# Slots, weight halves and token buffers at fixed places modulo 256 bytes

## The chip, the cores and the metric

One core of a Trainium2 chip runs the whole program. The metric is the device time of one execution in microseconds; the median of three runs stands for the kernel.

## The reference

The reference is one inference step of a decoder trunk with two layers, in float32, for a prompt of 512 tokens and for 8 sample tokens that share the weights. Each layer is a half-step SwiGLU feed-forward (FFN), a token mixer and another such FFN, each followed by a layer norm of `alpha*x + f(x)`.

```
swiglu_half(x) = 0.5 * ((silu(x @ wg) * (x @ wu)) @ wd)      # 1024 -> 2816 -> 1024
x = LN(alpha*x + swiglu_half(x))
x = LN(alpha*x + mixer(x))     # layer 0: retention (4 heads) beside RG-LRU; layer 1: causal pooling
x = LN(alpha*x + swiglu_half(x))
```

So there are four FFNs, one input and one output projection of the mixer of layer 0, and a small pooling mixer in layer 1. Outputs are the tokens and the new states.

## The kernel before, in words

Activations lie feature-major: 128 features of a chunk on the partitions, tokens along the free axis, 8 chunks. The 520 tokens are cut into two streams: stream 0 has the first 256 prompt tokens, stream 1 the other 256 and the 8 samples (`NN = (256, 264)`).

To keep float32 precision with fp32r products, each operand is split into a high part (rounded to fp32r) and a low part (the rest), and each product is made of three: high weight by high x, high weight by low x, low weight by high x (`emit`, line 533, calling `mm`, line 199; the matmuls stand at line 200). A unit of work is one output chunk of 128 columns: 8 (or 7) contraction chunks times three, so 24 (or 21) matmuls into one PSUM tile `ps`, for stream 0 with 256 columns and for stream 1 with 264. The two streams alternate, about six units apart, so each weight piece serves both.

The moving operands are of two kinds. For gate, up and mixer-input units they are the tiles `xh0`/`xh1` (high) and `xl0`/`xl1` (low), made in `alloc` (line 214) as constants of shape [128, 8, NN[s]]: a chunk stride of 1024 bytes in stream 0 and 1056 in stream 1. For down and mixer-output units they are hidden slots: `put_h` (line 846) and `ret_finish` (line 1138) take a slot as [128, 4, 264], rows high, low, high, low of two chunks, 1056 bytes apart in both streams (`hview`, line 836). In the rows below, xh and xl name the first kind, and `ps<-sl,sl` the second.

All slots are buffers of one pool of 36, each 1056 float32 wide (4224 bytes a partition), taken from its start by `slot` (line 119). A weight piece is up to 1024 float32 wide; it is loaded by a DMA from the SyncE queue into a slot (`load`, line 415), split in `prep` (line 427) into a high slot by ScalarE (line 178) and a low slot by VectorE (line 183), and then the raw slot is dropped. The order of the work is made at build time by a planner (`run`, line 501): it estimates the engines' times, and hands out slots by count. The number of slots that weights may hold (`wcap`, line 388) is the slot count less 10 in the FFNs, and a constant in the mixer and around the pooling; other work may take a slot when `can` (line 135) leaves a reserve.

The places in a partition follow from these sizes. The constants end at byte 57,920, so slot k starts at 57,920 + 4224k: 64 mod 256 for even k, 192 for odd k. The four x tiles start at 18,816, 27,008, 35,456 and 43,648, all 128 mod 256; stream 0's chunks all stay at 128, stream 1's step by 32. The chunks of a weight piece are 512 bytes apart. "Place 192/64" below says where high and low slot of a piece start, mod 256. The trace itself holds no addresses.

Of the kernel before, what the change touches and what calls it, by code (L numbers as in the profile page):

```python
# [8 lines left out]
F32 = mybir.dt.float32  # L9
F32R = mybir.dt.float32r  # L10
# [4 lines left out]
P = 128  # L15
DM = 1024
NCH = DM // P
# [4 lines left out]
NN = (HALF, HALF + NS)  # L22
# [15 lines left out]
QSCALE = 128.0 ** -0.5  # L38
GELU_C = math.sqrt(2.0 / math.pi)

NSLOT = 36
SLOTW = 1056
W_RESERVE = 5
N_RAW = 4
AHEAD = 5
# [46 lines left out]
class Build:  # L92
    def __init__(self, ctx, tc, ins, outs):
# [3 lines left out]
        self.cpool = ctx.enter_context(tc.tile_pool(name="cp", bufs=1))  # L97
        self.spool = ctx.enter_context(tc.tile_pool(name="sp", bufs=NSLOT))
        self.tpool = ctx.enter_context(tc.tile_pool(name="tp", bufs=2))
        self.pp = ctx.enter_context(tc.tile_pool(name="pp", bufs=5, space=bass.MemoryType.PSUM))  # L100
        self.pm = ctx.enter_context(tc.tile_pool(name="pm", bufs=3, space=bass.MemoryType.PSUM))
        self.free = NSLOT
        self.wused = 0
# [12 lines left out]
    def const(self, name, shape, dt=F32):  # L116
        return self.cpool.tile(shape, dt, tag=name, name=name)

    def slot(self, shape, dt=F32):
        assert self.free > 0, "no slot"  # L120
        self.free -= 1
        n = self.size(type("S", (), {"shape": shape}))
        assert n <= SLOTW
        t = self.spool.tile([P, SLOTW], dt, tag="slot", name=self.nm("sl"))
        v = t[:, :n]
        if len(shape) == 3:
            v = v.rearrange("p (a b) -> p a b", a=shape[1])
        elif len(shape) == 4:
            v = v.rearrange("p (a b c) -> p a b c", a=shape[1], b=shape[2])
        return v  # L130

    def drop(self, n=1):
        self.free += n
# [80 lines left out]
    def alloc(self):  # L214
        self.XE = [self.const(f"x{s}", [P, NCH, HALO + NN[s]]) for s in range(2)]
        self.XA = [t[:, :, HALO:] for t in self.XE]
        self.X = [[t[:, d, HALO:] for d in range(NCH)] for t in self.XE]
        self.XHA = [self.const(f"xh{s}", [P, NCH, NN[s]], F32R) for s in range(2)]
        self.XLA = [self.const(f"xl{s}", [P, NCH, NN[s]], F32R) for s in range(2)]
        self.XH = [[t[:, d, :] for d in range(NCH)] for t in self.XHA]  # L220
        self.XL = [[t[:, d, :] for d in range(NCH)] for t in self.XLA]
        self.H = [[None] * 4, [None] * 4]
        self.PT = [Tm(0.0), Tm(0.0)]
        self.SA, self.QA, self.M0, self.VA = [None] * 2, [None] * 2, [None] * 2, [None] * 2
        self.sm = self.const("small", [P, SMALL_W])
        self.ones_r = self.const("ones_r", [P, P], F32R)
        self.TL = self.const("tail", [P, NCH, PB + NS])
        self.XSM = self.const("xsm", [P, NCH, NS])
        self.b3 = self.const("b3", [P, NCH])
        self.UTAIL = self.const("utail", [P, 4, 3])  # L230
        self.UEND = self.const("uend", [P, 4, 3])
        self.HTAIL = [self.const(f"htail{s}", [P, 4]) for s in range(2)]
        self.US = self.const("us", [P, 4, NS])
        self.HS = self.const("hs", [P, 4, NS])
        self.SMP = self.const("smp", [P, 4, HEADS, NS])
        self.sp4 = self.const("sp4", [P, 4])
        self.pbs = self.const("pbs", [P, NCH])
        self.pss = self.const("pss", [P, NCH])
        self.one = self.const("one", [P, 1])
        self.tiny = self.const("tiny", [P, 1])  # L240
# [147 lines left out]
    def wcap(self):  # L388
# [4 lines left out]
        if self.idx[0] >= self.u_pool - 4 and self.idx[1] < self.u_pool + 8:  # L393
            return WCAP_P
        return NSLOT - WFF

# [30 lines left out]
    def prep(self, win=None):  # L427
        for wi, k in self.wanted(win or AHEAD + 1).items():
            if self.free < 2 or self.wused >= self.wcap():
                break  # L430
            w = self.wl[wi]
            if w["st"] != 1:
                continue
            if k > 0 and win is None and max(self.t_act, self.t_dve) > self.t_pe + 4.0:
                break
            T = Tm(w["traw"])
            if "full" in w:
                w["t"] = T.t
                w["st"] = 2
                self.nraw -= 1  # L440
                continue
            w["hi"] = self.slot([P, w["n"]], F32R)
            w["lo"] = self.slot([P, w["n"]], F32R)
            self.wused += 2
            raw = w["raw"][:]
            with self.prio(self.d_prep()):
                for c in range(0, w["n"], w["part"]):
                    cs = slice(c, c + w["part"])
                    self.act(T, w["hi"][:, cs], raw[:, cs])
                    if w is self.wl[0] and c == 0:  # L450
                        self.split(0, 0, Tm(0.0))
                    self.tt(T, w["lo"][:, cs], raw[:, cs], w["hi"][:, cs].bitcast(F32), ALU.subtract)
            w["t"] = T.t
            w["raw"] = None
            w["st"] = 2
            self.drop()
            self.wused -= 1
            self.nraw -= 1
            self.dma_ahead()
# [376 lines left out]
    def hview(self, s, k):  # L836
        t = self.H[s][k // 2]
        n = NN[s]
        j = 2 * (k % 2)
        return t[:, j, :n], t[:, j + 1, :n]  # L840

    def hfree(self, s):
        self.H[s] = [None] * 4
        self.drop(4)

    def put_h(self, T, s, k, h):
        if self.H[s][k // 2] is None:
            self.H[s][k // 2] = self.slot([P, 4, NN[1]], F32R)
        hi, lo = self.hview(s, k)
        self.act(T, hi, h)  # L850
        self.tt(T, lo, h, hi.bitcast(F32), ALU.subtract)
# [286 lines left out]
    def ret_finish(self, pr, s, T):  # L1138
        n = NN[s]
        B = self.RP[s]  # L1140
        yield from self.get(1)
        Q = self.slot([P, 4, NN[1]])
        ob, vv = B[:, 0:2, :n], B[:, 2:4, :n]
        sq, r0 = Q[:, 0:2, :n], Q[:, 2:4, :n]
        self.act(T, sq, ob, AF.Square)
        yield from self.pmget(2)
        yield ("pe", T)
        for e in range(2):
            pv = self.pmt()
            self.mm(pv[:, :n], self.s("ones"), sq[:, e, :], True, True)  # L1150
            T.t = self.t_pe + .1
            self.ts(T, vv[:, e, :], pv[:, :n], LN_EPS, ALU.add)
        self.pmfree += 2
        self.rstd(T, vv, r0, sq, vv)
        self.tt(T, ob, ob, vv, ALU.mult)
        yield ("v", None)
        while any(("sg", 2 * pr + e, s) not in self.flags for e in range(2)):
            yield ("w", None)
        yield from self.get(1)
        H = self.H[s][pr] = self.slot([P, 4, NN[1]], F32R)  # L1160
        for e in range(2):
            h = 2 * pr + e
            gn = self.s("gn_g")[:, h:h + 1]
            self.stt(T, ob[:, e, :HALF], ob[:, e, :HALF], gn, self.QK[h, s][:, 3, :], ALU.mult, ALU.mult)
            if s == 1:
                self.stt(T, ob[:, e, HALF:], ob[:, e, HALF:], gn, self.SMP[:, 3, h, :], ALU.mult, ALU.mult)
        hv = H[:, :, :n].rearrange("p (c two) n -> p two c n", two=2)
        hi, lo = hv[:, 0], hv[:, 1]
        self.act(T, hi, ob)
        self.tt(T, lo, ob, hi.bitcast(F32), ALU.subtract)  # L1170
        self.drop(4)
        if s == 1:
            self.drop(1 + pr)
        for h in (2 * pr, 2 * pr + 1):
            self.flags[("ret", h, s)] = T.t
            if s == 1:
                self.flags[("retdone1", h, 0)] = 0.0
                self.flags[("retdone1", h, 1)] = 0.0
# [235 lines left out]
```

## Time and profile before

| | us |
|---|---|
| three runs | 1850.99, 1851.36 (median), 1856.78 |
| profiled execution | 1856.6 |
| its span | 1854.8 |
| TensorE busy | 1816.8 (14727 matmul records) |
| VectorE busy | 909.8 |
| ScalarE busy | 688.3 |

The span runs from the first to the last instruction; a few us lie around it. Busy TensorE is not TensorE at its peak: records of matmuls overlap in time, and what counts is the distance from one start to the next. A window of one group (24 or 21 matmuls of one `ps` tile) has the group's first start and the next group's first start as its edges, so its length over 24 or 21 is that distance; its count of records is two higher than the group's, for the two matmuls before that are still in flight.

### The profile page before, as it was taken

To read this page: it belongs to the slowest core of one execution; us is meant where nothing else is said; L and a number is where in the kernel's file an instruction comes from. 1 tells how busy PE (TensorE), PEld (TensorE's weight loads), DVE (VectorE), ACT (ScalarE), POOL (GpSimd) and SP (SyncE) were. 2 spreads that over 40 slices of the span, in tenths; PEclk is the share of its full clock that TensorE was granted. 3 is DMA by queue.
4 is the path that set the end of the run, shared out by engine and by line. 5 is a ranking of instruction groups with operands and counts; after the bars stand their busy time and mean duration, and the time that the engine had idled before them with its cause. 6 is when DMAs were issued, how large, how long until landed. Compare 5 with 4: busy or idle time off the path is not lost.

```text
span 1854.8 us, 33820 instructions
## 1 busy us (share of the span) xinstructions
PE 1816.8 (98%) x14727; PEld 1791.7 (97%) x14727; DVE 909.8 (49%) x1629; ACT 688.3 (37%) x1208; POOL 2.1 (0%) x10
## 2 busy tenths in 40 slices
PE   8999999999899999999999999999999899999997
PEld 8999999999889999999999999999999799999997
DVE  5433333497655784333335833333347843333336
ACT  5422222275644463222223732222224742222223
POOL 0000000000000000000000000000000000000000
PEclk9999999999889999999999999999999999999998
DMA  7232232223043323222332323323259723223311
GB/s 259 92 92 86 87 102 84 76 80 103 13 146 97 126 82 92 92 86 90 99 89 85 113 81 93 96 85 100 77 80 97 71 84 99 91 84 99 96 31 47
DMA packets 77380, 170.74 MB, mean 92 GB/s; under 512 B 24368, under 2 KB 37168, under 8 KB 77232
## 3 DMA queue, kind: packets, MB, share of 16 engines
q1 hardware_dynamic: 77232, 168.58, 32.6%
q8 instruction: 115, 1.88, 0.4%
q14 instruction: 33, 0.27, 0.0%
HBM read 163.44 MB, written 5.12 MB: 91 GB/s over the span
## 4 chain that ended last, share of the span: by engine, by line
PE 88%; DVE 5%; ACT 5%; issue 1%; DMA 0%; SPq 0%; ACTq 0%; DVEq 0%
PE ps L200 85%; PE pm L200 3%; ACT sl L178 2%; DVE sl L183 2%; DVE sl L196 1%; DVE x L183 1%; ACT L685 1%; ACT L178 1%; ACT xh L178 1%; DVE xl L183 0%; DVE e L183 0%; DMA x<-in_xa 0%; ACT e L178 0%; ACT x L178 0%; DVE sl L968 0%
## 5 line engine op out<-in xcount | busy, mean ns | idle before, releaser
L200 PE MATMUL ps<-xh,sl 128*128 128x264 f32 (+1 forms) x6400 | 1177.1, 283 | 10.2 <-ACT xh L178 6.3
L200 PEld LDWEIGHTS ps<-xh,sl 128*128 128x128 f32 x6400 | 1000.1, 190 | 14.7 <-ACT xh L178 7.0
L200 PE MATMUL ps<-xl,sl 128*128 128x264 f32 (+1 forms) x3200 | 906.4, 284 | 3.6 <-DVE xl L183 3.3
L200 PEld LDWEIGHTS ps<-xl,sl 128*128 128x128 f32 x3200 | 607.3, 190 | 6.1 <-DVE xl L183 5.4
L200 PE MATMUL ps<-sl,sl 128*128 128x264 f32 (+1 forms) x4672 | 596.5, 285 | 4.1 <-DVE sl L196 4.0
L200 PEld LDWEIGHTS ps<-sl,sl 128*128 128x128 f32 x4672 | 577.3, 189 | 9.1 <-DVE sl L196 5.3
L178 ACT ACTIVATE sl<-sl 128x1024 fp32r<-128x1024 f32 (+8 forms) x371 | 349.0, 950 | 465.3 <-PE ps L200 421.2
L183 DVE TENSOR_TENSOR sl<-sl,sl 128x1024 fp32r<-128x1024 f32 (+3 forms) x320 | 374.1, 1174 | 243.3 <-ACT sl L178 222.9
L183 DVE TENSOR_TENSOR e<-sil,ps 128x256 f32<-128x256 f32 (+1 forms) x176 | 74.7, 424 | 305.4 <-PE ps L200 301.6
L196 DVE SCALAR_TENSOR_TENSOR x<-ps,x 128x256 f32<-128x256 f32 (+1 forms) x208 | 88.5, 427 | 249.1 <-PE ps L200 249.0
L178 ACT ACTIVATE sl<-e 128x264 fp32r<-128x264 f32 (+1 forms) x184 | 76.6, 416 | 282.5 <-DVE e L183 281.5
L178 ACT ACTIVATE sil<-ps 128x264 f32<-128x264 f32 (+1 forms) x176 | 67.1, 382 | 191.5 <-PE ps L200 190.8
L183 DVE TENSOR_TENSOR sl<-e,sl 128x264 fp32r<-128x264 f32 (+1 forms) x184 | 78.6, 427 | 60.2 <-ACT sl L178 60.1
L183 DVE TENSOR_TENSOR x<-x,sl 128x512 f32<-128x512 f32 (+2 forms) x136 | 87.1, 677 | 2.9 <-ACT sl L178 1.9
L178 ACT ACTIVATE e<-x 128x256 f32<-128x256 f32 (+1 forms) x87 | 35.1, 415 | 54.0 <-DVE x L196 53.7
L178 ACT ACTIVATE xh<-x,small 128x256 fp32r<-128x256 f32 (+1 forms) x64 | 35.1, 596 | 9.6 <-DVE x L183 9.5
L178 ACT ACTIVATE sl<-pm 128x256 f32<-128x256 f32 (+2 forms) x44 | 15.0, 364 | 57.7 <-PE pm L200 57.7
L183 DVE TENSOR_TENSOR xl<-x,xh 128x512 fp32r<-128x512 f32 (+1 forms) x40 | 27.6, 695 | 5.8 <-ACT xh L178 5.3
L183 DVE TENSOR_TENSOR sl<-sl,e 128x256 f32<-128x256 f32 (+1 forms) x63 | 26.8, 425 | 3.5 <-ACT e L178 2.2
L178 ACT ACTIVATE x<-x,small 128x256 f32<-128x256 f32 (+1 forms) x44 | 25.7, 596 | 4.5 <-DVE x L183 4.3
L178 ACT ACTIVATE e<-ps 64x256 f32<-64x256 f32 (+3 forms) x40 | 15.4, 384 | 26.2 <-PE ps L200 20.1
L183 DVE TENSOR_TENSOR sl<-sl,x 128x256 f32<-128x256 f32 (+1 forms) x54 | 23.0, 425 | 0.9
(115 smaller groups left out, 474.5 us busy)
## 6 DMA issues: line engine op xcount, KB each, us to landing
sl<-in_w SPq DMA_DIRECT2D x241, 512.0 KB, 3.7
sl<-in_w SPq DMA_DIRECT2D x64, 448.0 KB, 3.3
sl<-in_sret SPq DMA_DIRECT2D x4, 512.0 KB, 5.1
out_rets<-sl SPq DMA_DIRECT2D x4, 512.0 KB, 3.6
x<-in_xb SPq DMA_DIRECT2D x2, 528.0 KB, 9.2
out_y<-x SPq DMA_DIRECT2D x4, 264.0 KB, 2.3
x<-in_xa SPq DMA_DIRECT2D x4, 256.0 KB, 5.5
sl<-in_dec SPq DMA_DIRECT2D x2, 512.0 KB, 5.0
```

The source lines that it names most:

```text
L178: r = self.nc.scalar.activation(out, in_, func, scale=scale, **kw)
L183: r = self.nc.vector.tensor_tensor(out=out, in0=a, in1=b, op=op)
L196: self.nc.vector.scalar_tensor_tensor(out=out, in0=a, scalar=s, in1=b, op0=op0, op1=op1)
L200: self.nc.tensor.matmul(out, lhsT, rhs, start=start, stop=stop)
L685: self.nc.scalar.preload_act_table_set(LNEXP)
```

## The change

Slots become 1088 float32 wide (4352 bytes) and are 35 instead of 36. `slot` takes an offset. A high weight starts 32 float32 into its slot, a low one at its start. The x tiles of the high and low parts get chunk strides of 256 and 320 float32 (1024 and 1280 bytes). Hidden slots get row strides of 256 float32 at an offset of 16 in stream 0, and 264 at no offset in stream 1. The work itself, its engines and its shapes are the same.

```diff
--- before.py
+++ after.py
@@ -38,8 +38,12 @@
 QSCALE = 128.0 ** -0.5
 GELU_C = math.sqrt(2.0 / math.pi)
 
-NSLOT = 36
-SLOTW = 1056
+NSLOT = 35
+SLOTW = 1088
+XSTR = (256, 320)
+HSTR = (256, 264)
+HOFF = (16, 0)
+HIOFF = 32
 W_RESERVE = 5
 N_RAW = 4
 AHEAD = 5
@@ -116,18 +120,21 @@
     def const(self, name, shape, dt=F32):
         return self.cpool.tile(shape, dt, tag=name, name=name)
 
-    def slot(self, shape, dt=F32):
+    def slot(self, shape, dt=F32, off=0):
         assert self.free > 0, "no slot"
         self.free -= 1
         n = self.size(type("S", (), {"shape": shape}))
-        assert n <= SLOTW
+        assert off + n <= SLOTW
         t = self.spool.tile([P, SLOTW], dt, tag="slot", name=self.nm("sl"))
-        v = t[:, :n]
+        v = t[:, off:off + n]
         if len(shape) == 3:
             v = v.rearrange("p (a b) -> p a b", a=shape[1])
         elif len(shape) == 4:
             v = v.rearrange("p (a b c) -> p a b c", a=shape[1], b=shape[2])
         return v
+
+    def hslot(self, s):
+        return self.slot([P, 4, HSTR[s]], F32R, HOFF[s])
 
     def drop(self, n=1):
         self.free += n
@@ -215,8 +222,8 @@
         self.XE = [self.const(f"x{s}", [P, NCH, HALO + NN[s]]) for s in range(2)]
         self.XA = [t[:, :, HALO:] for t in self.XE]
         self.X = [[t[:, d, HALO:] for d in range(NCH)] for t in self.XE]
-        self.XHA = [self.const(f"xh{s}", [P, NCH, NN[s]], F32R) for s in range(2)]
-        self.XLA = [self.const(f"xl{s}", [P, NCH, NN[s]], F32R) for s in range(2)]
+        self.XHA = [self.const(f"xh{s}", [P, NCH, XSTR[s]], F32R)[:, :, :NN[s]] for s in range(2)]
+        self.XLA = [self.const(f"xl{s}", [P, NCH, XSTR[s]], F32R)[:, :, :NN[s]] for s in range(2)]
         self.XH = [[t[:, d, :] for d in range(NCH)] for t in self.XHA]
         self.XL = [[t[:, d, :] for d in range(NCH)] for t in self.XLA]
         self.H = [[None] * 4, [None] * 4]
@@ -439,7 +446,7 @@
                 w["st"] = 2
                 self.nraw -= 1
                 continue
-            w["hi"] = self.slot([P, w["n"]], F32R)
+            w["hi"] = self.slot([P, w["n"]], F32R, HIOFF)
             w["lo"] = self.slot([P, w["n"]], F32R)
             self.wused += 2
             raw = w["raw"][:]
@@ -845,7 +852,7 @@
 
     def put_h(self, T, s, k, h):
         if self.H[s][k // 2] is None:
-            self.H[s][k // 2] = self.slot([P, 4, NN[1]], F32R)
+            self.H[s][k // 2] = self.hslot(s)
         hi, lo = self.hview(s, k)
         self.act(T, hi, h)
         self.tt(T, lo, h, hi.bitcast(F32), ALU.subtract)
@@ -1157,7 +1164,7 @@
         while any(("sg", 2 * pr + e, s) not in self.flags for e in range(2)):
             yield ("w", None)
         yield from self.get(1)
-        H = self.H[s][pr] = self.slot([P, 4, NN[1]], F32R)
+        H = self.H[s][pr] = self.hslot(s)
         for e in range(2):
             h = 2 * pr + e
             gn = self.s("gn_g")[:, h:h + 1]
```

## Rows read from the trace of the kernel before

**Rows 1.** The profile page: engine shares, and TensorE's granted clock in 40 slices.
```profile
PE 1816.8 (98%) x14727; PEld 1791.7 (97%) x14727; DVE 909.8 (49%) x1629; ACT 688.3 (37%) x1208; POOL 2.1 (0%) x10
...
PEclk9999999999889999999999999999999999999998
```

**Rows 2.** The page's chain of waits, shares of the span by line.
```profile
PE ps L200 85%; PE pm L200 3%; ACT sl L178 2%; DVE sl L183 2%; DVE sl L196 1%; DVE x L183 1%; ACT L685 1%; ACT L178 1%; ACT xh L178 1%; DVE xl L183 0%; DVE e L183 0%; DMA x<-in_xa 0%; ACT e L178 0%; ACT x L178 0%; DVE sl L968 0%
```

**Rows 3.** Windows of FFN stretches: length; PE, PEld, DVE, ACT, POOL busy; clock, DMA share, GB/s.
```profile
60.00:340.00 280.00, 279.89 (x2353) 279.68 (x2352) 106.10 (x185) 78.14 (x122) 0.00 (x0) 1.00 0.29 89
...
700.00:1000.00 300.00, 300.00 (x2521) 300.00 (x2520) 112.53 (x170) 83.33 (x132) 0.00 (x0) 1.00 0.29 90
...
1530.00:1780.00 250.00, 250.00 (x2101) 250.00 (x2101) 89.68 (x134) 66.53 (x103) 0.00 (x0) 1.00 0.30 93
```

**Rows 4.** Windows, TensorE alone: one 256-column group on xh/xl each.
```profile
132.55:135.28 2.72, 2.72 (x26) 1.00 0.00 0
...
138.19:141.02 2.83, 2.83 (x26) 1.00 0.03 6
...
149.60:152.32 2.73, 2.73 (x26) 1.00 0.00 0
...
155.25:158.08 2.83, 2.83 (x26) 1.00 0.02 6
...
161.00:163.77 2.77, 2.77 (x26) 1.00 0.00 0
...
189.42:192.16 2.73, 2.73 (x26) 1.00 0.00 0
...
254.19:257.04 2.85, 2.85 (x26) 1.00 0.03 13
```

**Rows 5.** Groups by line and form: the fp32r products: busy, mean ns, idle before.
```profile
L200 PE MATMUL ps<-xh,sl 128*128 128x264 f32 x3200 | 616.3, 285 | 0.0
...
L200 PE MATMUL ps<-xh,sl 128*128 128x256 f32 x3200 | 596.2, 282 | 10.2 <-ACT xh L178 6.3 <-ACT sl L178 2.9 <-DVE sl L183 0.9
...
L200 PE MATMUL ps<-xl,sl 128*128 128x256 f32 x1600 | 451.5, 283 | 2.6 <-DVE xl L183 2.3
...
L200 PE MATMUL ps<-sl,sl 128*128 128x264 f32 x2336 | 304.8, 287 | 4.1 <-DVE sl L196 4.0
...
L200 PE MATMUL ps<-sl,sl 128*128 128x256 f32 x2336 | 301.2, 284 | 0.0
```

**Rows 6.** Windows of one 256-column group (21 matmuls) on hidden slots each.
```profile
212.07:214.58 2.50, 2.50 (x23) 1.00 0.00 0
...
222.91:225.36 2.45, 2.45 (x23) 1.00 0.00 0
...
233.64:236.15 2.51, 2.51 (x23) 1.00 0.06 24
```

**Rows 7.** Windows of one 264-column group each: three on xh/xl, the last on hidden slots.
```profile
163.77:166.67 2.90, 2.90 (x26) 1.00 0.51 158
...
169.42:172.34 2.92, 2.92 (x26) 1.00 0.59 163
...
186.53:189.42 2.89, 2.89 (x26) 1.00 0.50 159
...
241.54:244.12 2.58, 2.58 (x23) 1.00 0.58 167
```

**Rows 8.** Groups by line and form: the splits of a weight piece on VectorE and ScalarE.
```profile
L183 DVE TENSOR_TENSOR sl<-sl,sl 128x1024 fp32r<-128x1024 f32 x239 | 290.9, 1224 | 144.7 <-ACT sl L178 132.3 <-PE ps L200 11.8
...
L178 ACT ACTIVATE sl<-sl 128x1024 fp32r<-128x1024 f32 x239 | 249.9, 1055 | 323.5 <-PE ps L200 297.5 <-DVE sl L183 14.7 <-DMA sl<-in_w 11.2
```

**Rows 9.** Windows of the mixer stage.
```profile
400.00:500.00 100.00, 93.66 (x716) 90.56 (x715) 74.75 (x160) 65.66 (x124) 0.78 (x3) 0.95 0.14 49
...
500.00:600.00 100.00, 95.66 (x653) 87.96 (x652) 59.32 (x138) 45.52 (x98) 0.21 (x1) 0.90 0.37 118
```

## Prediction

> **What bounds the kernel now.** I read four views. [...] Then the chain of waits: TensorE's fp32r products (line 200 into ps) carry 85% of the span [rows 2]. So the time is, for the most part, a count of matmuls times the distance from one start to the next. Third, long FFN stretches with no stall: 280 us hold 2353 matmuls, 300 us hold 2521, 250 us hold 2101, which is 119.0 ns each [rows 3]. [...]
>
> Fourth, one output group per window. A group is 24 matmuls of one stream (8 chunks times three products); the count of 26 includes the last two of the group before, still in flight. All windows of rows 4 are the same form: 256 columns, moving operand xh or xl of the first half, clock 1.00, DMA share 0.00 to 0.03. Yet they take 2.72 to 2.85 us, that is 113.3 to 118.8 ns per matmul [rows 4]. What differs between them is which slots the weights lie in. The moving chunks of the first half start at 128 mod 256 bytes; a slot starts at 64 or at 192. From the order in which the program hands out slots, the high and low weights of the seven windows start at: 192/64 (132.55), 64/64 (138.19), 64/64 (149.60), 192/192 (155.25), 192/64 (161.00), 192/64 (189.42), 64/192 (254.19). Three places can do either: the two 64/64 windows show 117.9 and 113.8. Inside a group the starts hold a steady beat, quick (113.3 ns) or slow (117.8 or 118.8). 192/64 alone always ends in the quick beat, after at most nine matmuls of transition: 113.3, 115.4 and 113.8 ns here; over the whole trace the 42 such groups without a stall (the first starts at 15.4 us, the last at 1756.7) average 113.9, the other 135 about 116.2. DMA does not decide it: in the same trace matmuls with and without a transfer running differ by about 0.2 ns in each form.
>
> [...]
>
> **The change part by part.** Counts are from the groups by form: 3200 + 1600 matmuls of 256 columns on xh/xl, 2336 on hidden slots (32 of them are the pooling's), and the same again at 264 columns [rows 5].
>
> *Weight slots.* 4352 bytes is 17 times 256, so every slot starts at one place mod 256. The constants grow by 2 x 8 x 56 x 4 = 3584 bytes, 14 times 256, so that place is 64 as for slot 0 before. Low weights lie at 64, high ones 128 bytes on, at 192. This is the 192/64 place, for every piece. First half on xh/xl: the whole trace gives 115.9 ns before (the seven windows: 115.8); 113.9 plus the last transition into the next group is 114.2 after. 4650 undisturbed matmuls x 1.7 ns = 7.9 us gained.
>
> *Hidden slots, first half.* Before, the four rows of a slot are 1056 bytes apart from a start at 64 or 192, so starts wander over all places. The 21-matmul windows take 2.45 to 2.51 us, 116.7 to 119.5 ns [rows 6]; 118.4 over the trace. After, stride 1024 and offset 64 put every row at 128 mod 256: the same geometry as xh/xl, so I price it with the 192/64 rows, with a little more transition: 114.3. 2270 x 4.1 = 9.3 us gained.
>
> *Second half on xh/xl, 264 columns.* Before, chunks shift by 32 bytes mod 256 from one to the next; after, stride 1280 puts all eight at 128. The windows give 120.4 to 121.7 ns [rows 7], 121.1 over the trace. No row shows 264 columns at one place for a whole group. [...] Upper bound: the slowest row at 264 columns, 2.58/21 = 122.9. What speaks for the upper half: the first three matmuls of such a group do lie at 128, and in the window at 163.77, which is in place 192/64 and follows a quick group, their starts go 118, 121 and 121 ns apart in the records: the quick beat is left at once. So I take 120.7, near the rows: 4740 x 0.4 = 1.9 us gained; the ends are 21 gained and 9 lost.
>
> *Second half on hidden slots.* Stride stays 1056, the start becomes 64 always. Before: 122.9 ns in the window shown [rows 7], 121.9 over the trace. Places still wander: nothing, at the nearest rows; 1 ns either way is 2.3 us.
>
> *One slot less (36 to 35).* The FFN cap on weight slots is the slot count less 10, so 26 becomes 25; the caps of the mixer and pooling stages are constants and stay. What hides this is the lead: the split on ScalarE sat idle 297.5 us until TensorE gave a slot free, so it is the buffers, filled far ahead, that set its pace, while TensorE waited only 0.9 us for low weights at this form [rows 5, 8]. In the stretches of rows 3 a piece is split some 30 us before its first use; a slot is about 3 us of that. Cost: nothing. If the cover were gone, a piece's two split operations (1.06 + 1.22 us) would be late at stage edges only: I keep 0 to 4 us. No instruction or DMA is added or taken away, and the operations on DVE and ScalarE keep their sizes; SP's and POOL's queues are as they were. What is late next, when the FFN runs faster, is nothing: ScalarE and DVE are at 28 and 38% there and DMA at 0.29 to 0.30 [rows 3].
>
> *What does not gain in full.* In the mixer TensorE waits for other engines (93.7 of 100 us busy, clock 0.95 and 0.90 [rows 9]); about one matmul in nine is there, and of its 1.8 us I take back 1. Where pauses move, half-speed stretches move too: the clock of 0.90 over 100 us cost about 10 us, so a few us either way.
>
> Sum: -7.9 - 9.3 - 1.9 + 1 = -18 us. Against the profiled execution (1856.6 us, span 1854.8) this is 1838.5. That execution is 5.2 us above the median of 1851.4, near the highest of the three runs; the forecast goes by the median: 1851.4 - 18 = 1833 us, own range 1827 to 1841.
>
> **The rivals.**
> 1. *The second half falls into the quick beat as well.* With all chunks at one place its geometry is that of the first half. For: 192/64 draws in 256-column groups from any entry. Against: the 118, 121, 121 above. At 117 to 118.5 ns it gives 12 to 19 us in place of 1.9: about 1819 us.
> 2. *Slower: one place, but the wrong beat.* A fixed layout gives all groups one fate. If the entry from the changed 264-column groups locks the first half in the slow beat of 254.19 (118.8 ns), xh/xl lose 2.9 x 4650 = 13.5 us and hidden slots 0.4 x 2270 = 1: 1866 us. It decides when more than half of the groups lock (4.8 x 6920 ns = 33 us between none and all, against 18). Against: every 192/64 group of before came in from a 264-column one, in many phases, and none stayed slow.
> 3. *The places are not what I work out*, so that high and low lie at 64/192: xh/xl keep their 115.8, hidden slots gain about 2.6 ns: 1845 us. For: the trace shows no addresses. Against: both growths are multiples of 256.
> 4. *Addresses do not matter*, and the beats of before had another cause that followed the slots by chance: 1851 us, at most 4 more for the slot.
>
> **How the numbers follow.** Forecast 0.58, rival 1 0.22, rival 2 0.06, rival 3 0.08, rival 4 0.06. 0.3% is 5.6 us; a measurement here can hardly tell less from no change. Faster by more: the forecast and rival 1, rival 3 mostly (1845 is 6 us), 0.87. Within it: rival 4 and the rest of 3, 0.07. Slower: 0.06. The range takes in rival 1 to 1814 and rival 3 to 1847.
>
> **What would show it.** In the profile after: windows of one first-half group at 2.72 to 2.75 us in every FFN, on xh/xl and on hidden slots alike (24 matmuls), none at 2.83; the mean of one 256-column MATMUL down from 282 and 284 ns by some 3; stall-free FFN stretches at 117.6 ns per matmul (2380 in 280 us) instead of 119.0. Second-half xh/xl windows at 2.80 us would be rival 1. Wrong would be: first-half groups at 2.83 or more in steady state (rival 2), a mix of both as before (4), or TensorE waits for splits in the FFN (the slot).

## The result: slower, 1873.7 us against 1854.0

Four runs of the changed kernel gave a median of 1873.68 us (1868.27 to 1878.83), four of the kernel before beside them 1853.96; the ratio is 1.0106, 95% interval 1.0071 to 1.0142. The forecast was 1833 us, its range ended at 1847. The profiled execution of after took 1873.2 us, span 1871.5, against 1856.6 and 1854.8 before: 16.7 us of span to explain.

Two things happened at once. First, the places did what was forecast. Windows of one group each of after, TensorE alone (columns as in [rows 4]): three 256-column groups that follow a hidden 264-column group, one that follows a 264-column group on xh/xl, and then two 264-column groups, on hidden slots and on xh/xl:

```profile
131.54:134.28 2.74, 2.74 (x27) 1.00 0.51 145
137.22:139.95 2.73, 2.73 (x26) 1.00 0.33 126
142.89:145.62 2.73, 2.73 (x26) 1.00 0.30 60
205.10:207.87 2.77, 2.77 (x26) 1.00 0.28 61
128.60:131.54 2.94, 2.94 (x26) 1.00 0.04 14
207.87:210.76 2.89, 2.89 (x27) 1.00 0.25 100
```

The first-half group no longer takes 2.83 or 2.85 us as three of seven did in [rows 4]. From start to start of neighbouring matmul records, with distances above 135 ns counted as pauses (at a granted clock of 0.50 starts lie 220 ns apart, as from 338.3 to 342.7 us in after, and so count as pauses too), the whole trace gives (ns; number undisturbed in after):

```
                     before   after   undisturbed   change, us
256 on xh/xl         115.88   114.70      4655         -5.5
256 on hidden        118.36   115.13      2248         -7.3
264 on xh/xl         121.12   120.33      4677         -3.7
264 on hidden        121.95   122.21      2283         +0.6
pauses, in excess      41.7     73.9  (us)            +32.2
```

Matmuls that run undisturbed became 15.9 us cheaper, and pauses 32.2 us dearer: 16.3 of the 16.7 us.

Second, the pauses. Two FFN windows of after (columns as in [rows 3]):

```profile
100.00:350.00 250.00, 245.40 (x2052) 244.47 (x2051) 86.83 (x138) 64.47 (x105) 0.00 (x0) 0.99 0.28 88
700.00:1000.00 300.00, 295.43 (x2480) 294.64 (x2479) 101.69 (x158) 78.53 (x126) 0.00 (x0) 0.99 0.28 89
```

The second held 2521 matmuls, all of it busy, in [rows 3]; now it holds 2480. The page of after, shares, clock and chain of waits; before, the chain was 85% line 200 into ps (207 in after) and no load of weights stood among its lines [rows 1, 2]:

```profile
PE 1812.7 (97%) x14727; PEld 1784.1 (95%) x14727; DVE 894.7 (48%) x1629; ACT 683.1 (37%) x1209; POOL 3.4 (0%) x10
...
PEclk9999999999889999999999999999999999999998
...
PE ps L207 59%; DMA sl<-in_w 14%; ACT sl L185 7%; DVE sl L190 7%; PE pm L207 3%; DVE sl L203 2%; DVE x L190 1%; ACT L692 1%; DVE e L190 0%; ACT L185 0%; DVE x L203 0%; ACT e L185 0%; DVE xl L190 0%; DVE sl L975 0%; ACT xh L185 0%
```

Groups by line and form of after, against [rows 8, 5]: ScalarE's idle time before a 1024-wide split used to end with TensorE (297.5 of 323.5 us), and now ends with the load:

```profile
L185 ACT ACTIVATE sl<-sl 128x1024 fp32r<-128x1024 f32 x239 | 251.0, 1055 | 416.0 <-DMA sl<-in_w 393.5 <-PE ps L207 15.9 <-DVE sl L190 6.4
L185 ACT ACTIVATE sl<-sl 128x896 fp32r<-128x896 f32 x64 | 61.0, 953 | 182.0 <-DMA sl<-in_w 169.4 <-PE ps L207 12.6
...
L190 DVE TENSOR_TENSOR sl<-sl,sl 128x1024 fp32r<-128x1024 f32 x239 | 291.5, 1224 | 397.8 <-ACT sl L185 392.1 <-PE ps L207 5.3
...
L207 PE MATMUL ps<-sl,sl 128*128 128x256 f32 x2336 | 297.8, 282 | 13.6 <-ACT sl L185 13.3
```

The last line had no idle time at all in [rows 5].

**The loop.** The chain of waits of after in the stretch 818 to 850 us, in order of time (start, length, what), shows what ScalarE waits for:

```profile
821.82 3.55 DMA sl<-in_w
...
825.45 1.07 ACT sl L185
826.52 0.02 issue
826.54 1.25 DVE sl L190 x2
827.80 3.70 DMA sl<-in_w
...
831.52 1.07 ACT sl L185
832.59 0.02 issue
832.61 1.23 DVE sl L190
833.84 0.03 DVE e L190
833.86 3.33 DMA sl<-in_w
...
837.27 0.96 ACT sl L185
838.23 0.02 issue
838.26 1.09 DVE sl L190
839.35 0.03 DVE e L190
839.38 3.38 DMA sl<-in_w
```

Read it as a circle. A load starts within 0.03 us after VectorE has finished the split of the piece before, lands, is split on ScalarE and on VectorE, and only then the next load starts. One turn takes 5.98 and 6.06 us for a 1024-wide piece, 5.52 for an 896-wide one. TensorE uses up a 1024-wide piece in 48 matmuls, 24 x (114.7 + 120.3) ns = 5.64 us, and an 896-wide one in 42, 21 x (115.1 + 122.2) ns = 4.98 us. The circle is slower than both, so where it is closed ScalarE and VectorE fall behind TensorE from piece to piece. TensorE does not feel this at once: in the window that holds these turns it is busy without a break (columns as in [rows 3]).

```profile
820.00:860.00 40.00, 40.00 (x342) 40.00 (x341) 12.61 (x20) 11.51 (x21) 0.00 (x0) 1.00 0.27 85
```

Why it is closed follows from the order in which the program hands out slots. A loaded piece sits in a raw slot until its two splits are done. Before, 159 of the loads took the raw slot that the split two pieces back had left: two pieces per turn of the circle. After, 142 loads take the slot of the split directly before. The waits of the SyncE queue, on which loads are issued, fit this. First those of before, then of after (line waited for: us, times, longest). In after the queue reaches a load while the piece before is still on its way into the slot, and so waits first for that landing (the 146) and then for the splits:

```profile
SPq L419 <- DVE sl L183: 867.7, 177, 18.9
SPq L419 <- PE ps L200: 384.3, 66, 18.2
```
```profile
SPq L426 <- PE ps L207: 465.8, 84, 19.2
SPq L426 <- DMA sl<-in_w: 453.9, 146, 4.7
SPq L426 <- DVE sl L190: 284.4, 84, 25.3
```

What a late split costs is best seen at 337 us, in the chain of after again. The piece loaded at 330.64 has its split on ScalarE at 334.00 and on VectorE at 334.98. Behind the latter stands, on VectorE, the product of gate and up (e), and only then can ScalarE split that hidden tile (336.78), which TensorE's next products read:

```profile
330.64 3.27 DMA sl<-in_w
...
334.00 0.96 ACT sl L185
...
334.98 1.43 DVE sl L190 x2
336.41 0.34 DVE e L190
...
336.78 0.42 ACT sl L185
337.20 0.04 issue
337.25 1.92 PE ps L207 x6
```

And the windows around it, with the granted clock in the third column from the right:

```profile
325.00:333.00 8.00, 8.00 (x70) 8.00 (x69) 2.83 (x6) 1.92 (x4) 0.00 (x0) 1.00 0.33 108
333.00:338.00 5.00, 1.77 (x11) 1.41 (x11) 2.19 (x4) 1.68 (x3) 0.00 (x0) 0.80 0.20 49
338.00:343.00 5.00, 5.00 (x24) 5.00 (x24) 1.43 (x2) 1.65 (x3) 0.00 (x0) 0.52 0.13 53
343.00:350.00 7.00, 7.00 (x62) 7.00 (x61) 4.46 (x9) 2.64 (x6) 0.00 (x0) 1.00 0.34 82
```

TensorE stands for some 3.2 us, and then runs 5 us at a granted clock of 0.52, 24 matmuls where 42 would fit: that second part costs about 2 us and appears in no wait. The weights were not late: by the same trace a piece's split still ended some 25 to 35 us before its first use in the FFNs. What was late here were the small operations that stood behind a split, and that split had stood waiting for its load.

### The profile page after: what moved, and what is told of

Read it like the earlier page. It is cut to its first block, busy times and chain, and to the rows that moved or that the text cites. A ratio compares the mean times of both kernels' runs of the same rounds, so it can differ in the third digit from the quotient of the medians.

```text
span 1871.5 us, 33732 instructions
## 1 busy us (share of the span) xinstructions
PE 1812.7 (97%) x14727; PEld 1784.1 (95%) x14727; DVE 894.7 (48%) x1629; ACT 683.1 (37%) x1209; POOL 3.4 (0%) x10
## 4 chain that ended last, share of the span: by engine, by line
PE 62%; DMA 14%; DVE 11%; ACT 9%; issue 2%; SPq 0%; ACTq 0%; DVEq 0%
PE ps L207 59%; DMA sl<-in_w 14%; ACT sl L185 7%; DVE sl L190 7%; PE pm L207 3%; DVE sl L203 2%; DVE x L190 1%; ACT L692 1%; DVE e L190 0%; ACT L185 0%; DVE x L203 0%; ACT e L185 0%; DVE xl L190 0%; DVE sl L975 0%; ACT xh L185 0%
## 5 line engine op out<-in xcount | busy, mean ns | idle before, releaser
L207 PE MATMUL ps<-xh,sl 128*128 128x264 f32 (+1 forms) x6400 | 1173.6, 284 | 11.4 <-ACT xh L185 6.9
L207 PEld LDWEIGHTS ps<-sl,sl 128*128 128x128 f32 x4672 | 572.4, 189 | 29.4 <-ACT sl L185 16.4
L185 ACT ACTIVATE sl<-sl 128x1024 fp32r<-128x1024 f32 (+8 forms) x371 | 350.3, 951 | 612.5 <-DMA sl<-in_w 564.9
L185 ACT ACTIVATE sl<-pm 128x256 f32<-128x256 f32 (+2 forms) x44 | 15.1, 364 | 58.8 <-PE pm L207 58.8
```

The source lines that it names most:

```text
L185: r = self.nc.scalar.activation(out, in_, func, scale=scale, **kw)
L207: self.nc.tensor.matmul(out, lhsT, rhs, start=start, stop=stop)
```

## The experiments

Ratios are against the kernel before on the same chip. "Cap" is the number of slots that weights may hold in the FFN, the slot count less WFF (10): 26 before, 25 after. A first theory (A), held for the first four runs, was that at a cap of 25 loads are issued too late ahead of their splits, and that late loads cost. The rivals were that the new places themselves cost (B), that 35 slots are too few (C), and, for e4, that only an odd or even cap counts (D).

**e1: after with the cap put back to 26.**

```diff
-WFF = 10
+WFF = 9
```

> The changed kernel with one constant different: weights may hold 35 - 9 = 26 slots in the FFNs, as before the change, in place of 25. Theory A (a load comes too late): with 25 the planner issues a piece's load 2.6 us of its own time before the piece's split instead of 7.9 us, the load takes 3.6 us to land, ScalarE's in-order queue stands at the split and what is behind it reaches TensorE late. With 26 the distance is 7.9 us again, so this run keeps the 16 us that the new places gain between undisturbed starts and loses the stalls: 1837 us, 1832 to 1842. Rival B (the new places themselves cost, in DMA or ScalarE): stays at 1868 to 1879. Rival C (35 slots in all are too few, whatever the cap): 1865 or more.

Measured: 1840.35 us, ratio 0.9916 (0.9891 to 0.9940). The load's row among ScalarE's waits falls from 564.9 to 15.1 us, starts stay at 114.71, 115.12, 120.32 and 122.23 ns, and the excess of pauses is 44.8 us, near before's 41.7. The same windows of this kernel:

```profile
100.00:350.00 250.00, 250.00 (x2121) 250.00 (x2120) 93.74 (x147) 69.84 (x108) 0.00 (x0) 1.00 0.28 90
700.00:1000.00 300.00, 300.00 (x2546) 300.00 (x2545) 112.45 (x175) 84.48 (x132) 0.00 (x0) 1.00 0.29 90
```

So one slot more for weights, out of the same 35, gives the whole loss back, and the places are worth some 13 to 16 us. Rivals B and C are out. This version beats both kernels. Its loads follow neither of the two orders above; most now take slots that TensorE has left, as the SyncE queue's first row says:

```profile
SPq L426 <- PE ps L207: 1148.4, 225, 16.9
```

**e2: before with cap 25 out of 36 slots.**

```diff
-WFF = 10
+WFF = 11
```

> The kernel before with one constant different: weights may hold 36 - 11 = 25 slots in the FFNs in place of 26; places and slot sizes as before. Theory A: the loads come 2.6 us ahead of the split as in the changed kernel, so it loses what that one loses by stalls, without the gain: 1853 + 36 = 1889 us, 1878 to 1895, with ScalarE waiting some 500 us for loads. Rival B (the new places cost): 1853, no change. Rival C (35 slots in all): 36 slots are there, so no change.

Measured: 1856.64 us, ratio 1.0019 (1.0010 to 1.0029). Theory A missed by 32 us: ScalarE waits for loads 145 times here too, but only 2 to 5 us are lost. ScalarE's row:

```profile
ACT sl L178 <- DMA sl<-in_w: 270.5, 145, 5.1
```

A wait is 1.9 us long in the mean, in after 3.5 (564.9 / 162). Only 4 loads take the slot of the split directly before here; most go to slots that TensorE left. Late loads alone did little harm here.

**e3: before with 35 slots, cap 26 kept.**

```diff
-NSLOT = 36
+NSLOT = 35
-WFF = 10
+WFF = 9
```

> The kernel before with 35 slots, and the weights' cap in the FFNs kept at 26 (35 - 9): one slot less without the later loads, at the old places. Theory A: no change, 1853 us within 4. Rival C (35 slots in all are too few): slower by 20 us or more. Rival B says nothing against no change.

Measured: 1857.69 us, ratio 1.0022 (1.0008 to 1.0037). Rival C, 20 us or more, is out: a slot less in the pool costs some 4 us, 7 at most by the interval.

**e4: after with cap 24.**

```diff
-WFF = 10
+WFF = 11
```

> The changed kernel with the weights' cap at 35 - 11 = 24. The planner then issues every second load at the same moment as its split and the others 2.6 us ahead. Theory A: the wait of each second split grows from about 1 to 3.6 us and more, so slower than the changed kernel: 1885 us or more, ScalarE's wait for loads over 600 us. Rival D (what counts is only whether a raw piece is held over, by odd or even cap): as with 26, about 1837 us.

Measured: 1842.05 us, ratio 0.9941 (0.9923 to 0.9959). Theory A had foreseen at least 1885 and fell with this: with even fewer slots for weights the FFN windows are full again (2121 and 2546 matmuls). Here 81 loads take the slot of the split directly before, about every second one, so that two pieces share a turn. Rival D's time, about 1837 us, is met within 5 us, but an odd or even cap is not the cause by itself: e2 has the odd cap of 25 and loses 2 to 5 us. What goes with the loss in e1 to e4 is not how many weights are held, but which slot the next load falls into.

**e5: before with one slot less and nothing else: 35 slots, cap 25, old places.**

```diff
-NSLOT = 36
+NSLOT = 35
```

> The kernel before with only the slot taken away (35 slots, FFN cap 25; its old strides and places). Theory: the loss comes from the cap of 25 together with 25 + 10 = 35 slots, whatever the places are: loads are issued only one operation ahead of their split, and the slot they write has only just been given free. Then this kernel loses what the changed one lost, some 25 to 33 us: 1885 us (1875 to 1895), ScalarE waits some 500 us for in_w, and FFN stretches show fewer matmuls than 2521 in 700:1000. Rival: the loss needs the new places, whose quicker beat gives ScalarE less time: no more than 1862 us here, and 300 us hold 2521 matmuls as before.

Measured: 1868.86 us, ratio 1.0094 (1.0066 to 1.0122). Same order of slots as after (142 loads behind the split directly before), and the same wait:

```profile
ACT sl L178 <- DMA sl<-in_w: 545.7, 162, 6.0
```

The loss comes without the new places, so the rival is out; its size, 17 us, is below the 25 to 33 expected. The slower TensorE of this layout (5.69 us for a 1024-wide piece) is nearer to the circle's turn; that this makes the loss smaller is argued and not shown. Its windows:

```profile
100.00:350.00 250.00, 248.40 (x2086) 248.00 (x2085) 89.16 (x142) 65.73 (x107) 0.00 (x0) 1.00 0.28 91
700.00:1000.00 300.00, 298.01 (x2491) 297.61 (x2490) 105.10 (x166) 79.43 (x129) 0.00 (x0) 0.99 0.28 89
```

**e6: after, cap 25, with loads allowed one slot earlier everywhere** (in `dma_ahead`, which issues loads ahead of their splits).

```diff
-            if self.nraw >= N_RAW or self.free <= 0 or self.wused >= self.wcap() - 2:
+            if self.nraw >= N_RAW or self.free <= 0 or self.wused >= self.wcap() - 1:
```

> The changed kernel with its 35 slots and its FFN cap of 25, but a load may be issued at one slot less free (cap - 1 in place of cap - 2). Theory: the loss is the load issued too late ahead of its split, so it goes: 1840 us (1833 to 1846), ScalarE's waits for in_w fall from 565 us to under 50, FFN stretches as at cap 26 (2546 matmuls in 700:1000). Rival: the missing slot itself is what hurts (too few weights held ahead): 1873 us as it is.

Measured: 1849.42 us, ratio 0.9985 (0.9975 to 0.9995). ScalarE's wait for loads is 16.4 us and the FFN windows are full (2122 and 2546), as the theory says, but the time is 9 us above e1: above the theory's range, and far below the rival's value. The condition holds for the mixer as well; there this kernel is behind. First e6, then e1:

```profile
600.00:680.00 80.00, 70.58 (x522) 67.10 (x522) 55.42 (x111) 43.11 (x82) 0.00 (x0) 0.87 0.32 100
```
```profile
600.00:680.00 80.00, 79.09 (x608) 76.02 (x607) 69.58 (x135) 49.70 (x94) 0.00 (x0) 0.96 0.30 101
```

**e7: after with cap 26, second half's xh/xl at the old stride.**

```diff
-XSTR = (256, 320)
+XSTR = (256, 264)
...
-WFF = 10
+WFF = 9
```

> The changed kernel at FFN cap 26, with the second half's xh/xl at the old chunk stride of 264 elements (chunks shift by 32 bytes mod 256). Theory of places: only 264-column matmuls on xh/xl move, from 120.3 back to 121.1 ns, 4677 of them: 3.7 us more than at cap 26, 1844 us; 256-column ones stay at 114.7 and 115.1 ns. Rival (the second half's gain came from elsewhere): 120.3 stays and the time is 1840 us.

Measured: 1837.39 us, ratio 0.9919 (0.9900 to 0.9938): no more than e1. The 264-column starts went to 120.98 ns as expected, 3.1 us lost. The other half of the expectation missed: the 256-column groups got quicker, 114.13 on xh/xl and 114.18 on hidden slots, 4.9 us gained. They enter from another 264-column group; over the quick beat of 113.3 ns a group of 24 on xh/xl has 24 x 1.4 = 34 ns in e1 and 24 x 0.8 = 20 ns here, and that this is a shorter transition is an estimate from these means. The change's stride of 320 is not shown to be worth anything in sum.

**e8: after with cap 26, high weights at place 64 like the low ones.**

```diff
-HIOFF = 32
+HIOFF = 0
...
-WFF = 10
+WFF = 9
```

> The changed kernel at FFN cap 26, with the high weights at the same place mod 256 as the low ones (64 and 64 in place of 192 and 64). Theory of places: the first half's groups end in either beat or stay in the slow one; on xh/xl 116.2 ns (113.8 to 118.8) in place of 114.7, hidden slots the same: some 10 us more than at cap 26, 1850 us (1840 to 1868). Rival (the place of the weights is indifferent, only the strides of the tokens count): 114.7 and 115.1 ns stay, 1840 us.

Measured: 1855.37 us, ratio 1.0014 (1.0000 to 1.0027). All but 2 of the 282 first-half groups that ran in one piece now stay in the slow beat, 117.75 ns on xh/xl and 117.70 on hidden slots. Two windows of such groups:

```profile
139.02:141.85 2.83, 2.83 (x27) 1.00 0.55 152
...
207.77:210.60 2.83, 2.83 (x27) 1.00 0.52 144
```

Same instructions and order as e1, the clock at 1.00 in these windows, and 128 bytes in the place of one weight tile make up to 0.1 us a group and 15 to 18 us in all (by the medians and by the ratios to before). The prediction's second rival, one place but the wrong beat, exists: at 64/64, not at 192/64. The prediction's fourth rival, that addresses do not matter, is out by this.

**e9: as e6, but loads earlier in the FFN alone.**

```diff
-... self.wused >= self.wcap() - 2:
+... self.wused >= self.wcap() - (1 if self.wcap() == NSLOT - WFF else 2):
```

> The changed kernel, cap 25, with loads issued at one slot less free in the FFN alone (in the mixer and pooling stages as in the changed kernel). Theory: with cap 25 each load goes into the slot that the split just before it on VectorE gives free, so load, ScalarE's split and VectorE's split follow one another in a loop of 5.5 to 6.1 us a piece, while TensorE needs 48 matmuls, 5.6 us, for a piece; earlier loads land in slots that TensorE has left, and the loop is open. The 9 us that the earlier loads cost in all stages belong to the mixer. Then 1840 us (1834 to 1846). Rival: the missing slot costs them: 1849 us.

Measured: 1842.22 us, ratio 0.9930 (0.9912 to 0.9947). Met: 35 slots and a cap of 25 cost nothing once the load does not go into the slot of the split directly before (one load does).

**e10: after, cap 25, with high weights at place 64.**

```diff
-HIOFF = 32
+HIOFF = 0
```

> The changed kernel, cap 25, with the high weights at place 64 as well, which slows TensorE's first half to 117.7 ns a matmul. Theory of the loop (load, split, split): it sets the pace of the FFN, so a slower TensorE costs next to nothing here: 1873 us (1866 to 1880), ScalarE still waits over 450 us for in_w. Rival (stalls that add to TensorE's own time): 1874 + 15 = 1889 us (1883 to 1895).

Measured: 1879.94 us (1877.22 to 1882.98), ratio 1.0134 (1.0116 to 1.0153). It lies between the two: inside the loop's range, at its upper end, and 9 us below the rival's value. Against after (1.0106) the slower places cost 0.3%, against 1.0% at cap 26 (e8 over e1), so by the medians the circle hides most of it, though the intervals leave half of that open. One profiled execution of each pair says otherwise: 30.9 us of span between after and e1, 30.2 between e10 and e8. Matched matmul by matmul, these traces show where the time goes. In the down stretches with 896-wide pieces (groups of 21) after falls behind e1 by 30 us, and in all other stages by less than 1 in sum. In the same stretches e10 falls behind e8 by 25, and by another 8 in the mixer's output projection, for which no run gives a cause. So in the FFN of these executions the circle hides some 6 us of what the slower places cost.

**e11: after with cap 26, hidden slots in their old layout.**

```diff
-HSTR = (256, 264)
-HOFF = (16, 0)
+HSTR = (264, 264)
+HOFF = (0, 0)
...
-WFF = 10
+WFF = 9
```

> The changed kernel at cap 26 with the hidden slots' old layout (rows 264 apart from the slot's start) in both halves. Theory of places: the first half's 256-column matmuls on hidden slots go back from 115.1 to about 118.4 ns, 2271 of them: 7.4 us more than at cap 26, 1847 us; xh/xl stay at 114.7. Rival (only the weights' places count): 115.1 stays, 1840 us.

Measured: 1846.58 us, ratio 0.9955 (0.9938 to 0.9972). Met: 118.59 ns on hidden slots, 114.81 on xh/xl; the first half's hidden layout is worth 7 us.

**e12: after with cap 26, second half's xh/xl 128 bytes on, at place 0** (in the two lines that make XHA and XLA, shown as far as they differ).

```diff
+XOFF = (0, 32)
...
-WFF = 10
+WFF = 9
...
-... F32R)[:, :, :NN[s]] ...
+... F32R)[:, :, XOFF[s]:XOFF[s] + NN[s]] ...
```

> The changed kernel at cap 26 with the second half's xh/xl moved by 128 bytes, from place 128 to place 0 mod 256, stride 1280 kept. If the place of the moving operand decides as it does at 256 columns, the 264-column matmuls on xh/xl leave 120.3 ns, to some value from 117 to 122.5 that no run so far gives: 1825 to 1850 us. Rival (at 264 columns only the columns count): 120.3 and 1840 us.

Measured: 1839.49 us, ratio 0.9919 (0.9903 to 0.9936), 120.21 ns. Rival met: place 0 of the 264-column operand is no better than place 128 (120.32 ns in e1). e1, e7 and e12 have overlapping intervals; of the three none is shown to be the best.

## Why the prediction was wrong

**The step that failed is "One slot less": "Cost: nothing", with 0 to 4 us kept.** It measured 17 us at the old places (e5) and 33 us at the new ones (after against e1, of medians). The second rival had forecast a slower kernel too, 1866 us, but by the slow beat; the first-half groups of after are quick, so its nearness to 1874 is chance. The step looked for the cost in the amount held: weights are split 30 us ahead, a slot is 3 us of that. The amount was indeed no problem (e3: some 4 us; e4: within 2 us of e1; both with full windows). The cost lies in the order. 25 instead of 26 moved each load behind one more split, and with 35 slots the slot that comes free there is the raw one of that split. The rows shown as cover did not speak of this: "the split on ScalarE sat idle 297.5 us until TensorE gave a slot free" [rows 8] describes the order at cap 26, and the cap changes that order. The row that would have warned is the SyncE queue's, 867.7 us behind VectorE's splits in 177 loads: loads were already chained to splits, at two pieces per turn (11.4 us of TensorE's time for a chain of 6), and the only question was whether an edit would make it one per turn.

The prediction did list "TensorE waits for splits in the FFN (the slot)" among what would make it wrong, but gave it no price and no rival of its own. A price was at hand from rows of before: the two splits (1.06 + 1.22 us [rows 8]) and the load's median of 3.7 us from issue to landing, in the page's list of transfers, make 6.0 us, against 5.69 us of TensorE per piece. The row of before:

```profile
sl<-in_w SPq DMA_DIRECT2D x241, 512.0 KB, 3.7
```

**Weight slots: right in mechanism, too high in size.** Forecast 7.9 us, measured 5.5 in starts. 114.2 ns was too low, since it took the transition after a group from few windows: after a 264-column group on xh/xl it takes about ten matmuls every time (115.3 per group), after one on hidden slots three (114.0).

**Hidden slots, first half: right in mechanism, somewhat too high.** Forecast 9.3 us, measured 7.3 in starts and 7 in e11. 115.1 instead of 114.3 ns, for the same reason.

**Second half on xh/xl: right in sign, larger, and not its own.** Forecast 1.9 us, measured 3.7 in starts. But e7 shows that the 256-column groups pay it back: 114.71 ns on xh/xl in e1 against 114.13. No run shows the 21 us that the prediction gives as one end of this part; after, e1, e7 and e12 had 120.2 to 121.0 ns on xh/xl, at most 0.9 ns a matmul below before. First rival, the quick beat in the second half: out (120.3 ns in the mean, where it had 117 to 118.5, which no run shows as a mean; averaged by place in the group, starts lie 117 to 123 ns apart).

**Second half on hidden slots: nothing, as forecast** (+0.6 us).

**What the forecast would have been without the failed step:** e1 has all the places and no closed loop, and takes 1840 us, 13 to 16 us below the kernel before; the forecast of 18 us was some 2 to 5 us too high. It ends at the upper end of its own range, 1827 to 1841.

**What stays open.** That in the FFN a closed circle goes with the loss, and an open one with none, is shown (after, e5 and e10 against e1, e4 and e9). Why it costs 17 us at the old places and 33 at the new ones is only argued. The loss falls in the stretches of 896-wide pieces, where TensorE needs 4.98 us a piece in after, 5.02 in e10 and 5.05 in e5, against turns of some 5.5 us; the three lose 30, 25 and 14 us there (against e1, e8 and before). The order fits, but no run shows that differences this small make half of the loss. Nor was it tried why a given pair of places favours one beat; only that it does was shown.

## What to carry to other kernels

A buffer count decides not only how far ahead work is done, but which released buffer the next load gets. Before taking one buffer away, find what each load waits for in its queue's own waits; if it is an operation on the very piece before it, add load and both operations up and compare the sum with the time in which the consumer eats one piece. And the price of a late operand can be paid by whatever stands behind it on its engine: in the stall at 333 us VectorE idled 4.02 us before a split at 334.98, and the operations that ran next, without a break, were small ones on hidden tiles; TensorE waited for these, not for the weights.

## What the hardware showed that was not expected

- A 256-column fp32r matmul kept a beat of 113.3 ns or of 117.8 at a granted clock of 1.00 (2.72 and 2.83 us for 24 [rows 4]; moving operand at 128 mod 256 bytes). With the two weight tiles at 192/64 every undisturbed group of e1 reached the quick beat; at 64/64 all but 2 of 282 groups stayed slow in e8 and all but 13 of 281 in e10, so 64/64 can hold either. How many matmuls it took to reach the quick beat went with the group before: in after about ten behind a 264-column group on xh/xl and three behind one on hidden slots.
- At 264 columns the means were 120.2 to 121.1 ns on xh/xl (e12, e1, after, e7, before) and 121.95 to 122.23 on hidden slots (before, after, e1): in these kernels eight columns more cost 7 to 9 ns over the quick beat of 113.3.
- In after, at 333 us, a stall of TensorE of some 3.2 us was followed by about 5 us at a clock of 0.52.
